# Eight of each layer's 24 gate projections traced between the two rounds of the RWKV inverse's merge

## The chip, the core and the metric

The kernel runs on one NeuronCore of a Trainium2 chip. The metric is the device time of one execution in microseconds (us). A profile shows one execution on the chip with the engines PE (TensorE matmuls), PEld (its weight loads), DVE (VectorE), ACT (ScalarE), POOL (GpSimd) and SP, which issues the DMAs.

## The reference

Two layers of a diffusion backbone with 512 tokens (256 context, 256 latent), model width 1024, float32. Each layer is a half-step SwiGLU, a token mixing, and a second half-step SwiGLU. The mixing is what matters here:

```python
cols = split(h @ w_in)                  # one projection feeds three branches and the gates
A = bidirectional retention(8 heads)    # "ret"
B = windowed attention(8 heads)         # "att"
C = bidirectional RWKV-7(8 heads)       # "rwkv", a scan with a state update per token
g = sigmoid(gate_logits)                # 3 x 1024 columns of the same projection
merged = g_ret * (ret @ w_ret) + g_att * (att @ w_att) + g_rw * (rwkv @ w_rwkv)
out = merged @ w_out
```

The gates depend on the normed input h alone. In layer 0 all 512 tokens are wanted; in layer 1 only the 256 latent ones, and the context enters only through states and keys.

## The kernel before

Activations lie with features on the partitions, so one 128-wide column block of a projection is a sum over eight 128x128 weight blocks. Each product is split in three (`mm3`: high weight by high and low activation, low weight by high activation), so a gate is 24 products, 512 columns wide in layer 0 and 256 wide in layer 1, into one of the two `mm` banks of PSUM. Then ACT takes the tanh (L589) and SP stores it to DRAM (L590, tile `gd`). `Weights.get` brings the weights in loads of four blocks; ACT rounds them (L114, `whi`, four buffers) and DVE subtracts for the low part (L115, `wlo`, three buffers).

The RWKV scan is done in chunks of 64 tokens, for four pairs of heads `p` and the two halves `s` (context 0, latent 1). Its steps have letters in the table `ORDER`, which gives the order in which the mixing is traced:

- `c`: the pair's columns r, k and v, with their convolution (on DVE), and the norm of k.
- `A` (s = 0) and `C` (s = 1): `rw_prep`. Its last score products (L976) give small triangular matrices. POOL inverts their 32x32 diagonal blocks in 62 instructions (L1008, L1009), after a trip through DRAM, and SP sends the result through DRAM (L1012 `td`).
- `B` (s = 0) and `D` (s = 1): `rw_back`, which first merges the 32x32 blocks into 64x64 inverses (`rw_merge`): it reloads the blocks (L1018, tile `z`), transposes and copies them on DVE (L1023, L1027) and ACT (L1026), multiplies in a first round of 16 products 32x32 (L1035), copies the result on ACT (L1036, tile `xm`), and multiplies in a second round of 16 (L1040). Then come `rw_vals` (L1052) and the chain of state updates `rw_chain` (L1079 to L1107): PE, ACT and DVE in turn, four steps in two directions, whose L1086 reads the merged inverse.

The other letters are `P` and `H` (retention: projections and heads), `kv`, `q`, `t` (attention), and `G`, two gates. Here `B0` of layer 0 is written 0B0, and so on. A scheduler takes the traced instructions, goes by their order as a priority, and puts an instruction whose inputs come late behind others whose inputs are there. Each engine then works through its queue in the order so made. `tc.issue_after(x)` orders what is traced inside it behind instruction `x` where both are on one engine.

Of the kernel before, what the change touches and what calls it, by code (L numbers as in the profile page):

```python
# [26 lines left out]
G3 = 3  # L27
# [3 lines left out]
def fm(src, n0, k=KT, k0=0):  # L31
    return [(src, kt, n0) for kt in range(k0, k0 + k)]


def grp(src, n0):
    return [(src, kt, n0 + j) for kt in range(KT) for j in range(2)]
# [15 lines left out]

ORDER = ['lo c0 A0 C0 B0 P0 kv c1 D0 H0 H1 q0 A1 t0 P1 t1 G0 C1 B1 H2 G1 c2 H3 G2 D1 A2 G3 q1 B2 P2 G4 C2 H4 t2 G5 t3 c3 A3 G6 H5 D2 G7 G8 P3 H6 G9 C3 B3 H7 D3 G10 G11', 'lo c0 A0 C0 P0 H0 kv B0 D0 c1 A1 H1 q0 t0 G0 t1 C1 G1 B1 P1 c2 D1 H2 A2 H3 P2 C2 G2 G3 H4 G4 c3 q1 G5 t2 t3 G6 B2 H5 D2 G7 A3 C3 G8 P3 B3 G9 G10 H6 H7 D3 G11']


def plan_mix(l):
    r0 = RCOL // 128
    out = []  # L60
    for w in ORDER[l].split():
        k, j = w[0], w[1:]
        if w == "lo":
            out.append(("lo", [("mix", kt, r0 + 12 + j) for kt in range(KT) for j in range(3)]))
            if l > 0:
                out.append(("vd", [("vd", 0, 0), ("vd", 0, 1)]))
        elif k == "c":
            p = int(j)
            out += [(f"r{p}", fm("mix", r0 + p)), (f"k{p}", fm("mix", r0 + 4 + p)), (f"v{p}", fm("mix", r0 + 8 + p))]
        elif k == "P":  # L70
            p = int(j)
            out += [(f"rq{p}", fm("mix", p)), (f"rk{p}", fm("mix", 4 + p)), (f"rv{p}", grp("mix", 8 + 2 * p))]
        elif k == "H":
            out.append((f"rg{j}", fm("mix", 16 + int(j))))
        elif w == "kv":
            out.append(("akv", grp("mix", 28)))
        elif k == "q":
            out.append((f"aq{j}", grp("mix", 24 + 2 * int(j))))
        elif k == "G":
            out += [(f"g{g}", fm("mix", 45 + g)) for g in range(2 * int(j), 2 * int(j) + 2)]  # L80
    for n in range(KT):
        out.append((f"ba{n}", fm("watt", n, 4)))
    out += [(f"br{n}", fm("wret", n)) for n in range(KT)]
    out += [(f"bw{n}", fm("wrw", n, 4)) for n in range(KT)]
    out += [(f"wo{n}", fm("wout", n)) for n in range(KT)]
    return out
# [36 lines left out]
def body(nc, tc, I, O, es, dbg=None):  # L123
# [3 lines left out]
    V, A, G, PE, SP = nc.vector, nc.scalar, nc.gpsimd, nc.tensor, nc.sync  # L127

    def mk(shape, tag, bufs=1, dt=F32):
        return sb.tile(shape, dt, name=tag, tag=tag, bufs=bufs)  # L130
# [3 lines left out]
    def ps(tag):  # L134
        return pp.tile([128, 512], F32, name="ps_" + tag, tag=tag, bufs=NB[tag])
# [4 lines left out]
    def ft():  # L140
        return mk([128, 512], "ft", 8)
# [7 lines left out]
    def span(S):  # L149
        return slice(S[0] * 256, S[-1] * 256 + 256)  # L150
# [34 lines left out]
    def mm3(o, w, h, start, stop):  # L185
        PE.matmul(o, w[0], h[0], start=start, stop=False)  # L186
        PE.matmul(o, w[0], h[1], start=False, stop=False)  # L187
        PE.matmul(o, w[1], h[0], start=False, stop=stop)  # L188

    def rsqrt(y, x):  # L190
        p, n = x.shape
# [14 lines left out]
    st = {"apart": False}  # L206
# [120 lines left out]
    def hl(h, c):  # L327
        return h[0][:, c], h[1][:, c]

    def dense(W, key, H, c, o):  # L330
        bl = W.take(key)
        for j, t in enumerate(bl):
            mm3(o[:, c], W.get(t), hl(H[j], c), j == 0, j == len(bl) - 1)

    def last_out(W, key, H, gate):

# [243 lines left out]
        SP.dma_start(out=st["od"][8 + h, :, c], in_=g[:, c])  # L580


    def gates(W, H, j, S, st):
        c = span(S)
        for g in range(2 * j, 2 * j + 2):
            o = ps("mm")
            dense(W, f"g{g}", H, c, o)
            t = ft()
            A.activation(t[:, c], o[:, c], AF.Tanh, scale=0.5)  # L589
            SP.dma_start(out=st["gd"][g, :, c], in_=t[:, c])  # L590

    def spilled(st, j, n, S, dst, mark, scale=None):
        c = span(S)
        for p in range(n):
            t = ft()
            with tc.issue_after(mark):
                SP.dma_start(out=t[:, c], in_=st["od"][j + p, :, c])
            split(hl(dst[p], c), t[:, c], scale)
        return dst
# [412 lines left out]
            SP.dma_start(out=td[:, :, g], in_=tt[g * 32:g * 32 + 32])  # L1012
        X["td"] = td

    def rw_merge(X, st):
        z, tn, xm = mk([64, 2, 8, 32], "z", 2), mk([32, 16, 32], "rb", 3)[:, 0:8], mk([64, 16, 32], "rb", 3)[:, 0:8]
        for b in range(2):
            mark = SP.dma_start(out=z[32 * b:32 * b + 32].rearrange("p d u t -> p (d u) t"), in_=X["td"][16 * b:16 * b + 16].rearrange("u j g i -> (j g) u i")).ins  # L1018
        st["marks"].append(mark)
        fl = lambda t: t.rearrange("p u t -> p (u t)")  # L1020
        tg = X["tg"]
        tu = [tg[d].rearrange("p h c t -> p (h c) t") for d in range(2)]
        V.transpose(fl(tn), fl(z[0:32, 0]))  # L1023
        for b in range(2):
            bs = slice(32 * b, 32 * b + 32)
            A.copy(tu[0][bs, :, bs], z[bs, 0])  # L1026
            V.transpose(tu[1][bs, :, bs], z[bs, 1])  # L1027

        o = ps("rx")
        ov, o2 = (o[:, j * 256:j * 256 + 256].rearrange("p (u x) -> p u x", x=32) for j in range(2))  # L1030
        ab = (slice(0, 32), slice(32, 64))
        for d in range(2):
            a, b = ab[d], ab[1 - d]
            for u in range(8):
                PE.matmul(ov[b, u], X["off"][a, u], tn[:, u] if d == 0 else z[a, 1, u], start=True, stop=True)  # L1035
        A.copy(xm, ov[0:64])  # L1036
        for d in range(2):
            a, b = ab[d], ab[1 - d]
            for u in range(8):
                PE.matmul(o2[a, u], xm[b, u], tu[d][b, u, b], start=True, stop=True)  # L1040
        V.tensor_copy(tu[0][ab[0], :, ab[1]], o2[ab[0]])
        A.copy(tu[1][ab[1], :, ab[0]], o2[ab[1]])

# [97 lines left out]
    def rw_front(l, p, s, S, st):  # L1141
        R, X = st["rw", p]
        rw_prep(l, p, s, R, st, s in S, X[s])

    def rw_back(l, p, s, S, st):
        R, X = st["rw", p]
        rw_merge(X[s], st)
        rw_vals(s, R, st, s in S, X[s])
        ya = rw_chain(l, p, s, R, st, s in S, s == 0, X[s])
        if s in S:  # L1150
            rw_out(l, p, s, R, st, ya, X[s])
            if p < 3:
                SP.dma_start(out=st["od"][p, :, CS[s]], in_=R["r"][:, CS[s]])
            else:
                st["last"] = R["r"]
# [20 lines left out]
    def mix(l, W, H, S, vf, mark, st):  # L1176
        c = span(S)
        st["mark"] = mark
        st["od"] = dp.tile([16, 128, 512], F32, name="od", tag="od", bufs=2)
        st["gd"] = dp.tile([24, 128, 512], F32, name="gd", tag="gd", bufs=2)  # L1180
        for w in ORDER[l].split():
            k, j = w[0], w[1:]
            if w == "lo":
                rw_lora(W, H, l, S, st)
            elif k == "c":
                st["rw", int(j)] = rw_cols(W, H, l, int(j), S, st, vf), [{}, {}]
            elif k in "AC":
                rw_front(l, int(j), "AC".index(k), S, st)
            elif k in "BD":
                rw_back(l, int(j), "BD".index(k), S, st)  # L1190
            elif k == "P":
                ret_proj(W, H, int(j), S, st)
            elif k == "H":
                ret_head(W, H, int(j), S, st)
            elif w == "kv":
                att_kv(W, H, st)
            elif k == "q":
                att_q(W, H, int(j), S, st)
            elif k == "t":
                att_pair(int(j), S, st)  # L1200
            elif k == "G":
                gates(W, H, int(j), S, st)
        return branches(W, S, st), st["mark"]

    def mix_out(l, W, ms, S, xd):
# [21 lines left out]
    for l in range(2):  # L1227
        S = both if l == 0 else lat
# [4 lines left out]
        if l == 0:  # L1233
# [3 lines left out]
            H = norm(0, 0, 0, both, fine)  # L1237
            tk = tasks(0, range(2, 9))
        else:
            H = norm(1, 0, 0, both)  # L1240
            ada_cond()
            tk = tasks(1, range(5, 9))
        W = Weights(nc, mk, I[f"w{l}a"], plan_ffn("f1i", "f1o"))
# [4 lines left out]
        H = norm(l, 1, 3, both)  # L1248
        xd = dp.tile([8, 128, 512], F32, name="xd", tag="xd", bufs=2)
        for kt in range(KT):  # L1250
            mark = SP.dma_start(out=xd[kt], in_=xs[kt]).ins
        W = Weights(nc, mk, I[f"w{l}b"], plan_mix(l), True)
        ms, mark = mix(l, W, H, S, vf, mark, mst)
        mix_out(l, W, ms, S, xd)
        H = norm(l, 2, 6, S)
# [5 lines left out]
        W = Weights(nc, mk, I[f"w{l}c"], plan_ffn("f2i", "f2o"))  # L1261
# [105 lines left out]
```

## Time and profile before

| | |
|---|---|
| time, median of 3 runs | 2948.22 us (2942.67 to 2951.27) |
| the profiled execution | 2950.47 us, its span 2948.7 us |
| PE busy | 2797.0 us (95%), 16761 matmuls |
| DVE, ACT, POOL busy | 2002.5, 1319.8, 376.2 us |
| mean granted TensorE clock | 0.963 of full speed |

The span is the time from the first to the last instruction of the profiled execution. PE is busy for 95% of it, but "busy" counts a matmul at half clock for twice as long. The mean of the granted clock, 0.963, says how much of the span ran at which of the two levels.

### The profile page before, as it was taken

To read this page: it belongs to the slowest core of one execution; us is meant where nothing else is said; L and a number is where in the kernel's file an instruction comes from. 1 tells how busy PE (TensorE), PEld (TensorE's weight loads), DVE (VectorE), ACT (ScalarE), POOL (GpSimd) and SP (SyncE) were. 2 spreads that over 40 slices of the span, in tenths; PEclk is the share of its full clock that TensorE was granted. 3 is DMA by queue.
4 is the path that set the end of the run, shared out by engine and by line. 5 is a ranking of instruction groups with operands and counts; after the bars stand their busy time and mean duration, and the time that the engine had idled before them with its cause. 6 is when DMAs were issued, how large, how long until landed. Compare 5 with 4: busy or idle time off the path is not lost. (4 is left out here: it accounts for less than half of the span.)

```text
span 2948.7 us, 47410 instructions
## 1 busy us (share of the span) xinstructions
PE 2797.0 (95%) x16761; PEld 2389.1 (81%) x16761; DVE 2002.5 (68%) x4677; ACT 1319.8 (45%) x2968; POOL 376.2 (13%) x1068
## 2 busy tenths in 40 slices
PE   7999999889999999999999999999989889899999
PEld 6888888767877787788888888888878788788999
DVE  7977668676676666566756466465787767678655
ACT  3322245556555654333223232233567665565544
POOL 0000000522132112000000000000033434330000
PEclk9999999789999999999999999999999888899999
DMA  7655534212333136534534435343433234246554
GB/s 267 232 189 183 163 122 130 83 39 82 111 97 89 49 123 207 176 102 147 195 114 169 147 111 185 104 164 122 137 90 108 75 110 116 61 124 212 170 179 154
DMA packets 259727, 400.97 MB, mean 136 GB/s; under 512 B 78752, under 2 KB 96288, under 8 KB 259488
## 3 DMA queue, kind: packets, MB, share of 16 engines
q1 hardware_dynamic: 259488, 397.93, 42.2%
q8 instruction: 132, 2.16, 0.3%
q14 instruction: 107, 0.88, 0.1%
HBM read 368.33 MB, written 25.82 MB: 134 GB/s over the span
## 5 line engine op out<-in xcount | busy, mean ns | idle before, releaser
L114 ACT CAST whi<-raw 128x512 fp32r<-128x512 f32 x954 | 564.1, 618 | 675.7 <-PE ps_mm L187 350.0
L186 PE MATMUL ps_mm<-hall,whi 128*128 128x512 f32 (+1 forms) x2320 | 845.1, 365 | 10.2 <-DVE rr_v L801 4.0
L188 PE MATMUL ps_mm<-hall,wlo 128*128 128x512 f32 (+1 forms) x2320 | 842.6, 364 | 2.0 <-DVE wlo L115 2.0
L187 PE MATMUL ps_mm<-hall,whi 128*128 128x512 f32 (+1 forms) x2320 | 840.8, 363 | 0.0
L115 DVE TENSOR_TENSOR wlo<-raw,whi 128x512 fp32r<-128x512 f32 x954 | 643.8, 691 | 104.3 <-ACT whi L114 68.3
L186 PEld LDWEIGHTS ps_mm<-hall,whi 128*128 128x128 f32 x2320 | 442.9, 191 | 80.6 <-ACT cst L981 4.4
L188 PEld LDWEIGHTS ps_mm<-hall,wlo 128*128 128x128 f32 x2320 | 441.6, 191 | 74.8 <-DVE wlo L115 4.1
L187 PEld LDWEIGHTS ps_mm<-hall,whi 128*128 128x128 f32 x2320 | 442.0, 191 | 71.4 <-issue 0.2
L186 PE MATMUL ps_mm<-hid,whi 128*128 128x512 f32 (+1 forms) x737 | 260.6, 354 | 0.0
L187 PE MATMUL ps_mm<-hid,whi 128*128 128x512 f32 (+1 forms) x737 | 259.9, 354 | 0.0
L188 PE MATMUL ps_mm<-hid,wlo 128*128 128x512 f32 (+1 forms) x737 | 257.3, 354 | 0.0
L1008 POOL TENSOR_TENSOR cst<-acc,cst 128x60 f32<-128x60 f32 (+24 forms) x496 | 172.4, 348 | 615.5 <-DMA acc<-ad__10934 59.2
L401 DVE TENSOR_TENSOR ft<-ft,ps_mm 128x512 f32<-128x512 f32 (+1 forms) x80 | 49.7, 621 | 210.4 <-PE ps_mm L188 198.1
L373 DVE SCALAR_TENSOR_TENSOR x<-ps_mm,cst,x 128x256 f32<-128x256 f32 x136 | 61.0, 480 | 193.1 <-PE ps_mm L188 193.1
L853 POOL TENSOR_TENSOR ll<-lora,lh 128x512 fp32r<-128x512 f32 x8 | 10.3, 1282 | 1359.2 <-DVE ft L300 942.6
L1009 POOL TENSOR_TENSOR cst<-cst 128x60 f32<-128x60 f32 (+24 forms) x496 | 176.2, 355 | 38.1
L236 DVE SCALAR_TENSOR_TENSOR ft<-m,cd 128x1024 bf16<-128x1024 f32 x136 | 163.0, 1221 | 9.8 <-DMA m<-ada 9.8
L237 DVE SCALAR_TENSOR_TENSOR m<-m,cd 128x1024 f32<-128x1024 f32 x136 | 165.4, 1221 | 0.7
L186 PEld LDWEIGHTS ps_mm<-hid,whi 128*128 128x128 f32 x737 | 139.1, 189 | 19.6
L187 PEld LDWEIGHTS ps_mm<-hid,whi 128*128 128x128 f32 x737 | 139.1, 189 | 19.4
L188 PEld LDWEIGHTS ps_mm<-hid,wlo 128*128 128x128 f32 x737 | 138.5, 189 | 19.4
L187 PE MATMUL ps_mm<-wlo,hall 128*128 128x256 f32 x416 | 122.6, 295 | 2.7 <-DVE wlo L115 2.6
(339 smaller groups left out, 4505.3 us busy)
## 6 DMA issues: line engine op xcount, KB each, us to landing
m<-ada SPq DMA_DIRECT2D x136, 512.0 KB, 4.4
raw<-w0b SPq DMA_DIRECT2D x214, 256.0 KB, 2.9
raw<-w1b SPq DMA_DIRECT2D x211, 256.0 KB, 3.2
raw<-w0a SPq DMA_DIRECT2D x132, 256.0 KB, 2.8
raw<-w0c SPq DMA_DIRECT2D x132, 256.0 KB, 4.5
raw<-w1a SPq DMA_DIRECT2D x132, 256.0 KB, 4.3
raw<-w1c SPq DMA_DIRECT2D x132, 256.0 KB, 3.9
gd<-ft SPq DMA_DIRECT2D x24, 256.0 KB, 2.0
```

The costliest lines, as they stand in the source:

```text
L114: nc.scalar.copy(hi, raw)
L115: nc.vector.tensor_sub(lo, raw, hi.bitcast(F32))
L186: PE.matmul(o, w[0], h[0], start=start, stop=False)
L187: PE.matmul(o, w[0], h[1], start=False, stop=False)
L188: PE.matmul(o, w[1], h[0], start=False, stop=stop)
L236: V.scalar_tensor_tensor(junk, raw, 1.0, st["cond"][0], ALU.mult, ALU.mult, accum_out=md[:, kt, 0:1])
L237: V.scalar_tensor_tensor(raw, raw, 1.0, st["cond"][1], ALU.mult, ALU.mult, accum_out=md[:, kt, 1:2])
L373: V.scalar_tensor_tensor(xs[n][:, CS[s]], o[:, CS[s]], gate[:, n, s:s + 1], xs[n][:, CS[s]], ALU.mult, ALU.add)
L401: V.tensor_tensor(sg[:, c], sg[:, c], pu[:, c], ALU.mult)
L853: G.tensor_sub(ll, lw, lh.bitcast(F32))
L1008: G.tensor_tensor(w, acc[j // 16][:, j % 16, j + 1:32].unsqueeze(1).to_broadcast([128, m, n]), tt[:, 0:m, j:j + 1].to_broadcast([128, m, n ...
L1009: G.tensor_tensor(tt[:, 0:m, j + 1:32], tt[:, 0:m, j + 1:32], w, ALU.add)
```

## The change

`ORDER` keeps eight `G` of twelve in each layer, now numbered 4 to 11: layer 0 loses the four that stood at G0, G2, G5 and one of G7 and G8; layer 1 loses those at G0, one of G2 and G3, G5 and G7 (the numbers before). The gates 0 to 7 go to the merges: `rw_merge` calls `gate()` between its two rounds, which traces one gate's 24 products with its tanh and its store, and the second round is traced under `issue_after` of the last of these products. The order of the weights in DRAM (`plan_mix`) follows.

```diff
+        elif k in "GBD":
+            gs = range(2 * int(j), 2 * int(j) + 2) if k == "G" else [2 * int(j) + "BD".index(k)]
+            out += [(f"g{g}", fm("mix", 45 + g)) for g in gs]
...
-    def gates(W, H, j, S, st):
+    def gates(W, H, gs, S, st):
         c = span(S)
-        for g in range(2 * j, 2 * j + 2):
+        for g in gs:
             o = ps("mm")
-            dense(W, f"g{g}", H, c, o)
+            ins = dense(W, f"g{g}", H, c, o)
...
+        return ins
...
-    def rw_merge(X, st):
+    def rw_merge(X, st, gate):
...
         A.copy(xm, ov[0:64])
-        for d in range(2):
-            a, b = ab[d], ab[1 - d]
-            for u in range(8):
-                PE.matmul(o2[a, u], xm[b, u], tu[d][b, u, b], start=True, stop=True)
+
+        mark = gate()
+        with tc.issue_after(mark):
+            for d in range(2):
+                a, b = ab[d], ab[1 - d]
+                for u in range(8):
+                    PE.matmul(o2[a, u], xm[b, u], tu[d][b, u, b], start=True, stop=True)
...
-        rw_merge(X[s], st)
+        rw_merge(X[s], st, lambda: gates(W, H, [2 * p + s], S, st))
```

Two places in PE's queue show what the scheduler makes of it. The first is the merge 0B0. Before, these rows stand around its two rounds (`ps_rx<-rb,cst` and `ps_rx<-z,cst` are round one, `ps_rx<-tg,rb` round two, L976 the score products of 0C0, L559 a retention head):

```order
L188 MATMUL ps_mm<-whi,hall 128x256
L976 MATMUL ps_rf<-arz,kb 128x256 x2
L1035 MATMUL ps_rx<-rb,cst 32x32 x8
L1035 MATMUL ps_rx<-z,cst 32x32 x8
L1052 MATMUL ps_rx<-cst,rr_v 128x128 x2
L559 MATMUL ps_po<-ft 128x128 x2
L1040 MATMUL ps_rx<-tg,rb 32x32 x16
```

The rows 128x256 into `ps_mm` are the attention's query columns (q0); 48 of them stand ahead of round one. With the change, round one of 0B0 (now L1038) stands here, with the lines six numbers on (L561 for L559, L979 for L976):

```order
L979 MATMUL ps_rf<-arz,kb 128x256 x2
L188 MATMUL ps_mm<-hall,whi 128x512
L189 MATMUL ps_mm<-hall,wlo 128x512
L561 MATMUL ps_po<-ft 128x128 x2
L550 MATMUL ps_sc<-rqh,rks 128x512
L551 MATMUL ps_sc<-rql,rks 128x512
L979 MATMUL ps_rf<-arz,kb 128x256 x2
L1038 MATMUL ps_rx<-rb,cst 32x32 x8
L1038 MATMUL ps_rx<-z,cst 32x32 x8
L1058 MATMUL ps_rx<-cst,rr_v 128x128 x2
L187 MATMUL ps_mm<-whi,hall 128x256
```

No q0 product stands ahead of round one any more, and 32 of them stand between the rounds; the gate that 0B0 itself traces stands some 450 rows ahead, and that of 0D0 some 100 rows ahead.

The second place is the merge 1B2 in layer 1. Before, its two rounds follow each other, split only by score products of 1C2:

```order
L1134 MATMUL ps_rx<-cst,rb 128x64 x4
L1135 MATMUL ps_rx<-lo,cst 128x256
L1035 MATMUL ps_rx<-rb,cst 32x32 x8
L1035 MATMUL ps_rx<-z,cst 32x32 x8
L1040 MATMUL ps_rx<-tg,rb 32x32 x6
L976 MATMUL ps_rf<-arz,kb 128x256 x2
L1040 MATMUL ps_rx<-tg,rb 32x32 x10
```

With the change this is round one and what follows it (the products 128x512 are columns of pair 3):

```order
L1140 MATMUL ps_rx<-cst,rb 128x64 x4
L1141 MATMUL ps_rx<-lo,cst 128x256
L1038 MATMUL ps_rx<-rb,cst 32x32 x8
L1038 MATMUL ps_rx<-z,cst 32x32 x8
L979 MATMUL ps_rf<-arz,kb 128x256 x2
L187 MATMUL ps_mm<-hall,whi 128x512
```

and this is round two, 160 rows further on (the products into `ps_mm` ahead of it are the end of 1B2's gate):

```order
L737 MATMUL ps_ap<-cst,ft 128x128 x3
L189 MATMUL ps_mm<-hall,wlo 128x256
L187 MATMUL ps_mm<-hall,whi 128x256
L188 MATMUL ps_mm<-hall,whi 128x256
L189 MATMUL ps_mm<-hall,wlo 128x256
L1046 MATMUL ps_rx<-tg,rb 32x32 x16
```

Between them stand 24 products of 512 columns and 122 of 256, three gates among them.

## Rows read from the trace of the kernel before

**Rows 1.** The span by stretch (windows): busy time of each engine, granted clock, DMA.

```profile
410.00:1240.00 830.00, 772.11 (x4825) 641.47 (x4825) 569.94 (x1530) 438.36 (x1085) 183.84 (x532) 0.94 0.34 103
...
2065.00:2715.00 650.00, 588.84 (x4422) 517.04 (x4421) 477.84 (x1300) 393.06 (x996) 192.15 (x532) 0.92 0.38 112
```

**Rows 2.** Line L1040, the second round: what its engine sat idle for, times.

```profile
  ACT rb L1036: 1.0, 2
```

**Rows 3.** Tile z: what engines sat idle for, and who waited (us, times).

```profile
  DMA z<-td: 112.6, 33
...
  ACT tg L1026: 61.7, 19
```

**Rows 4.** Timeline of 0B0, from the last score product of 0A0 to round one.

```profile
509.11 1.02 PE L976 MATMUL ps_rf<-arz,kb 128*128 128x256 f32 x4
...
552.45 1.18 SPq L1018 DMA_DIRECT2D z<-td  x2
...
556.66 0.83 ACT L1026 COPY tg<-z 32x256 f32<-32x256 f32 x2 [10.66 <-DMA z<-td]
...
558.08 0.90 PE L1035 MATMUL ps_rx<-rb,cst 32*32 32x32 f32 x13 [7.57 <-DVE rb L1023]
```

**Rows 5.** Windows behind that wait, and of layer 1's worst stretch: columns as in rows 1.

```profile
560.00:580.00 20.00, 19.39 (x122) 17.94 (x123) 10.84 (x47) 9.26 (x32) 10.30 (x33) 0.57 0.27 73
...
558.00:616.00 58.00, 49.73 (x312) 42.31 (x312) 41.17 (x145) 32.22 (x94) 20.98 (x66) 0.71 0.20 55
...
2388.00:2460.00 72.00, 66.68 (x443) 59.74 (x442) 46.02 (x127) 41.52 (x108) 22.39 (x66) 0.82 0.36 103
```

**Rows 6.** Timeline of PE: the other stalls behind a late z.

```profile
881.61 0.68 PE L1107 MATMUL ps_rx<-ve,tg 64*64 64x64 f32 x4 [3.56 <-ACT ve L1088]
...
2197.86 0.56 PE L1035 MATMUL ps_rx<-rb,cst 32*32 32x32 f32 x13 [1.56 <-DVE rb L1023]
...
2328.89 0.55 PE L186 MATMUL ps_mm<-hall,whi 128*128 128x256 f32 x1 [4.01 <-DVE rr_v L801]
...
2383.65 0.56 PE L1035 MATMUL ps_rx<-rb,cst 32*32 32x32 f32 x13 [1.19 <-DVE rb L1023]
2387.48 1.22 PE L1052 MATMUL ps_rx<-cst,rr_v 128*128 128x128 f32 x4 [2.76 <-ACT kbT L958]
...
2518.47 0.66 PE L1079 MATMUL ps_rx<-cst,gk 128*64 128x128 f32 x2 [5.79 <-DVE cst L1102]
```

**Rows 7.** Timeline of PE: products in a row at full clock, and a head's.

```profile
511.01 0.48 PE L548 MATMUL ps_sc<-rqh,rks 128*128 128x512 f32 x1
...
511.56 0.28 PE L908 MATMUL ps_rf<-lw,lh 128*128 128x256 f32 x1
...
544.96 1.95 PE L559 MATMUL ps_po<-ft 128*128 128x128 f32 x16
...
548.42 0.28 PE L186 MATMUL ps_mm<-whi,hall 128*128 128x256 f32 x1
548.54 0.28 PE L187 MATMUL ps_mm<-wlo,hall 128*128 128x256 f32 x1
...
749.22 0.39 PE L186 MATMUL ps_mm<-hall,whi 128*128 128x512 f32 x1
749.45 0.39 PE L187 MATMUL ps_mm<-hall,whi 128*128 128x512 f32 x1
```

**Rows 8.** Timeline of DVE and POOL late in the inverse for 1D2.

```profile
2500.10 0.68 DVE L115 TENSOR_TENSOR wlo<-raw,whi 128x512 fp32r<-128x512 f32 x1
...
2500.11 0.84 POOL L1008 TENSOR_TENSOR cst<-acc,cst 128x65 f32<-128x65 f32 x1
...
2502.50 0.31 POOL L1008 TENSOR_TENSOR cst<-acc,cst 128x66 f32<-128x66 f32 x1
```

**Rows 9.** Timeline of PE around 1B2: round one and the chain's first step on the inverse.

```profile
2462.85 0.59 PE L1035 MATMUL ps_rx<-rb,cst 32*32 32x32 f32 x13
...
2487.61 0.44 PE L1086 MATMUL ps_rx<-cst,tg 64*64 64x64 f32 x4
```

More of the change, by code (lines that the diff above doesn't have):

```diff
@@ L49, in plan_ffn @@
     return out
-ORDER = ['lo c0 A0 C0 B0 P0 kv c1 D0 H0 H1 q0 A1 t0 P1 t1 G0 C1 B1 H2 G1 c2 H3 G2 D1 A2 G3 q1 B2 P2 G4 C2 H4 t2 G5 t3 c3 A3 G6 H5 D2 G7 G8 P3 H6 G9 C3 B3 H7 D3 G10 G11', 'lo c0 A0 C0 P0 H0 kv B0 D0 c1 A1 H1 q0 t0 G0 t1 C1 G1 B1 P1 c2 D1 H2 A2 H3 P2 C2 G2 G3 H4 G4 c3 q1 G5 t2 t3 G6 B2 H5 D2 G7 A3 C3 G8 P3 B3 G9 G10 H6 H7 D3 G11']
+ORDER = ['lo c0 A0 C0 B0 P0 kv c1 D0 H0 H1 q0 A1 t0 P1 t1 C1 B1 H2 G4 c2 H3 D1 A2 G5 q1 B2 P2 G6 C2 H4 t2 t3 c3 A3 G7 H5 D2 G8 P3 H6 G9 C3 B3 H7 D3 G10 G11', 'lo c0 A0 C0 P0 H0 kv B0 D0 c1 A1 H1 q0 t0 t1 C1 G4 B1 P1 c2 D1 H2 A2 H3 P2 C2 G5 H4 G6 c3 q1 t2 t3 G7 B2 H5 D2 A3 C3 G8 P3 B3 G9 G10 H6 H7 D3 G11']
 def plan_mix(l):
@@ L78, in plan_mix @@
             out.append((f"aq{j}", grp("mix", 24 + 2 * int(j))))
-        elif k == "G":
-            out += [(f"g{g}", fm("mix", 45 + g)) for g in range(2 * int(j), 2 * int(j) + 2)]
+        elif k in "GBD":
+            gs = range(2 * int(j), 2 * int(j) + 2) if k == "G" else [2 * int(j) + "BD".index(k)]
+            out += [(f"g{g}", fm("mix", 45 + g)) for g in gs]
     for n in range(KT):
@@ L187, in mm3 @@
         PE.matmul(o, w[0], h[1], start=False, stop=False)
-        PE.matmul(o, w[1], h[0], start=False, stop=stop)
+        return PE.matmul(o, w[1], h[0], start=False, stop=stop).ins
     def rsqrt(y, x):
@@ L332, in dense @@
         for j, t in enumerate(bl):
-            mm3(o[:, c], W.get(t), hl(H[j], c), j == 0, j == len(bl) - 1)
+            ins = mm3(o[:, c], W.get(t), hl(H[j], c), j == 0, j == len(bl) - 1)
+        return ins
     def last_out(W, key, H, gate):
@@ L590, in gates @@
             SP.dma_start(out=st["gd"][g, :, c], in_=t[:, c])
+        return ins
     def spilled(st, j, n, S, dst, mark, scale=None):
@@ L1143, in rw_front, with rw_back @@
         rw_prep(l, p, s, R, st, s in S, X[s])
-    def rw_back(l, p, s, S, st):
+    def rw_back(W, H, l, p, s, S, st):
         R, X = st["rw", p]
-        rw_merge(X[s], st)
+        rw_merge(X[s], st, lambda: gates(W, H, [2 * p + s], S, st))
         rw_vals(s, R, st, s in S, X[s])
@@ L1189, in mix @@
             elif k in "BD":
-                rw_back(l, int(j), "BD".index(k), S, st)
+                rw_back(W, H, l, int(j), "BD".index(k), S, st)
             elif k == "P":
@@ L1201, in mix @@
             elif k == "G":
-                gates(W, H, int(j), S, st)
+                gates(W, H, range(2 * int(j), 2 * int(j) + 2), S, st)
         return branches(W, S, st), st["mark"]
```

## The prediction

> **What bounds the kernel now.** I began with the busy time by stretch. TensorE is the bound nearly everywhere; only the two mixings leave it idle, 830 − 772.1 = 58 us in layer 0 and 650 − 588.8 = 61 us in layer 1, and there alone the mean granted clock is clearly under 1, at 0.94 and 0.92 [rows 1]. No product is added or taken away, so the change can win or lose only within these 119 us and in what the clock costs.
>
> Then I asked what the second round, which the change moves, waits for. The reader should see that it waits for almost nothing: ACT's copy L1036, the input that a gate between the rounds could cover, costs 1.0 us in the whole kernel [rows 2]. What engines do wait for in a merge stands ahead of both rounds: the reloaded blocks `z`, 112.6 us of idle time over all engines, 61.7 of it on ACT alone [rows 3]. Most of that is hidden from TensorE, but not all. At 0B0 the last score product leaves at 509.11, `z` is issued at 552.45, ACT's copy has waited 10.66 us for it and TensorE 7.57 us when round one starts at 558.08 [rows 4]. So 49 us pass, and where TensorE's own queue holds less than that, it stops.
>
> The remaining stalls of this kind are in the timeline: 3.56 (chain of 0B2), 1.56 (1B0), 4.01 (ahead of 1B1), 1.19 and 2.76 (1D1), 5.79 (the chain of the pair before, waiting for DVE, which stands at 1D2's `z`) [rows 6]. With the 7.57 they make 26.4 us. These are what the change can move: a gate placed ahead of round one is cover for `z`, one between the rounds or elsewhere is not.
>
> **The change part by part.** Moving eight gates per layer moves 24 products each, two roundings on ACT, two subtractions on DVE, a tanh and a store. Their count stays, so their own cost is nothing; they lie under TensorE's queue, and the store's tile `gd` is read only after the mixing.
>
> *The second round's new wait.* By name the change makes round two wait for a gate. In the order of the changed kernel the gate stands between the rounds in two of 16 merges, 0B3 and 1B2; in the other 14 it was put far ahead and round two is free at once. In 0B3 both kernels hold much work between the rounds. In 1B2 round two and what is queued behind it (`rw_vals`, the chain's first read of the inverse, L1086) come later: before, round one stood at 2462.85 and L1086 at 2487.61 [rows 9]; now 63 more products of 256 columns stand ahead of L1086, counted from 1A2's last score product, at 0.12 us (548.42 to 548.54) [rows 7], so 7.6 us. The chain itself loses the same 63 as cover (88 before, 25 now). Its end moves by nothing if that cover was not needed, and by up to 7.6 us if all of it was. I take 2.0, near the low end, since four steps still have some 20 us of attention products between them.
>
> *The cover of `z`.* I counted what stands between a merge's last score product and its round one, before and now, with prices at full clock: 0.23 us for 512 columns (749.22 to 749.45), 0.12 for 256, 0.55 for the pair L548/L549 (511.01 to 511.56), 1.95 / 16, about 0.11 less overlap, for L559 [rows 7].
> - 0B0: 23 more products of 512 (+5.3), 48 of 256 gone (−5.8), ten L559 gone (−1.1), three pairs gone (−1.65), small ones −0.4: 3.7 us less cover, so the wait of 7.57 grows to about 11.3.
> - 1B0: 18 products of 256 more and one pair less, +1.7: its 1.56 disappears.
> - 1B1: four pairs and eight L559 gone, 3.0 less; the stall of 4.01 grows by that.
> - 1D1: 75 products of 256 gone (−9.0), three pairs and eight L559 more (+2.5), small ones −0.4: 6.9 less; 1.19 becomes about 8.
> - 1D2: on DVE, whose wait matters here, `z` is met 3.7 us of TensorE work later, so 5.79 shrinks by 3.7.
> - 0B2: ACT meets `z` 7.2 us later, so its 3.56 disappears.
> - 1D3: 19 products of 256 less, 2.5 in all, against a present wait of under half a us: +2.5.
>
> *What is given back.* A product that leaves a cover stands somewhere else, and if it falls where TensorE idles, the wait that grew is paid back. Behind 0B0 there is plenty of room: from 558 to 616 us TensorE is busy 49.73 of 58, at a clock of 0.71 [rows 5], and the order puts 48 more products of 256 and ten more L559 here. 48 × 0.12 + 10 × 0.11 = 6.9 against 8.3 idle: I take all of the 3.7 as returned. Behind 1D1, 2388 to 2460 idles 5.3 of 72 us [rows 5]; I take half of 1D1's loss as returned, and half for 1B1 and 1D3, where no row decides between nothing and all.
>
> The sum: 0B0 0, 1B0 −1.6, 1B1 +1.5, 1D1 +3.5, 1D2 −3.7, 0B2 −3.6, 1D3 +1.3, 1B2 +2.0, together −0.6 us. The profiled execution took 2950.47 us, so 2949.9; it lies 2.25 above the median of the runs, so 2947.6, and I say 2948. That is no change: about 0.3%, or 8.8 us, is what a measurement of this kernel tells from none.
>
> **A rule weighed against the trace.** Late in an inverse POOL's 128x65 product took 0.84 us beside a subtraction L115 of 0.68, while a 128x66 one alone took 0.31 [rows 8]. So a gate's two L115 falling into an inverse could make its `z` later by 2 × 0.53, or at most by 2 × 0.68 = 1.4 us. The Trainium skill, "SBUF — State Buffer", section "SBUF: two separate sides", says that a VectorE operation with two SBUF inputs and a GpSimd operation hold their shared ports exclusively, the later one standing still for the whole instruction. By that rule 0.84 is nearly one L115 of waiting plus 0.31, and the trace agrees. Were each of 0B0, 1D1 and 1D3 to get 1.4, the sum would be −0.6 + 4.2, or 2952 instead of 2948. Subtractions of other columns fill those stretches in both kernels, so I do not add it.
>
> **The rivals.**
> - *Faster: the waits that grew are returned in full, and the clock stays up.* The three gains are 1.6 + 3.7 + 3.6 = 8.9, so 2939. Besides, behind 0B0's wait the clock falls: 560 to 580 has 0.57, with TensorE busy 19.39 [rows 5]. At 0.57 a share of 0.86 lies at the half level, and 19.39 × 0.86 / 2 = 8.3 us is what it costs. If the denser work there keeps the clock at 2.4 GHz, 2931. I take 2935. What speaks for it is that this stretch gets more products; against it, that the wait ahead of it is longer, and after such an idle time the clock fell. It decides at whether the granted clock in the 20 us behind 0B0's round one is above 0.8.
> - *Slower: nothing is returned.* Then 3.7 − 1.6 + 3.0 + 6.9 − 3.7 − 3.6 + 2.5 + 7.6 = +14.8, so 2963. The place is layer 1, where 1B2's chain hangs behind three gates: its late end makes the next pair's products late, and they stand ahead of 1D2's. For it speaks that the idle in 2388 to 2460 is in pieces, waits of chains among them, which a product from elsewhere doesn't fill. It decides at 1B2's chain ending more than about 4 us later against the work around it.
> - *The change doesn't do what it says:* the second round hardly waited and in 14 merges the gate isn't between the rounds. Then what remains is a re-ordering of gates, and the mechanisms above are all there is. I hold this as true in any case; it is why I forecast no change.
>
> **How the numbers follow.** No change, 2948, has a chance of 0.40; its own range, with each half returned between nothing and all, is 2939 to 2957. The faster rival has 0.33, the slower 0.27: the order was reshuffled at 14 places, and every term is a few us with either sign, so neither is far behind. From 2930 to 2963 the range takes in the full price of both rivals.
>
> **What would show it.** In the changed profile, round one of 0B0 should wait about 11 us (7.57 before), that of 1D1 about 8, and 1B0's 1.56, the 3.56 in 0B2's chain and most of the 5.79 should be gone. The second round (L1046) should still wait for next to nothing, also in 1B2, where it follows round one by some 25 us. TensorE's busy time at full clock must be the same. I am wrong if the idle time in the two mixings differs from 58 + 61 by more than 9 us, if the clock in either one moves by 0.02 (some 13 us), or if waits appear at other places than those listed, for instance at casts L114 held up in ACT's queue behind a `z` that now stands earlier among them.

## The result

The changed kernel takes 2973.33 us (median of 4 runs, 2966.28 to 2974.58) against 2948.77 before: a ratio of 1.0081, 95% interval 1.0059 to 1.0104. It is slower by 24 us, where no change was forecast, and outside the range of 2930 to 2963. Its profiled execution has a span of 2970.7 us.

The windows of the two mixings, cut at this kernel's own ends, answer to [rows 1] (columns as there):

```profile
410.00:1247.00 837.00, 784.90 (x4822) 652.94 (x4823) 570.02 (x1520) 432.50 (x1083) 185.22 (x532) 0.93 0.34 101
2074.00:2733.00 659.00, 580.59 (x4395) 510.64 (x4394) 471.93 (x1289) 388.26 (x993) 194.00 (x532) 0.92 0.38 111
```

Layer 0's mixing is 7 us longer, with 52 us of idle time instead of 58, so it lost to the clock. Layer 1's two windows do not end at the same place of the program. From the first score product (L976, now L979) to the last product of the RWKV output (L1135, now L1141) both do the same products:

```profile
2147.20:2710.20 563.00, 510.55 (x3909) 448.25 (x3908) 410.18 (x1135) 344.94 (x903) 186.95 (x525) 0.92 0.38 111
```

```profile
2156.20:2733.00 576.80, 507.28 (x3908) 446.80 (x3908) 407.63 (x1135) 341.62 (x903) 188.82 (x525) 0.92 0.38 108
```

The first line is before, the second after: 13.8 us longer, with 69.5 us idle instead of 52.5. The end of it moved by 23 us in all.

What the second round waits for, and what engines wait for at `z`, first looks unchanged. This is the line of the second round, as [rows 2]:

```profile
  ACT rb L1039: 1.8, 4
```

And this is tile `z`, as [rows 3], its time as a whole and who stood there:

```profile
  DMA z<-td: 116.0, 36
...
  ACT tg L1029: 56.5, 19
  DVE tg L1030: 36.8, 11
  DVE rb L1026: 22.6, 6
```

112.6 became 116.0 us (93.1 in a second execution, experiment 5, so this total says little by itself). But TensorE is hit harder by the same standing. These are its long stalls behind a late `z` in the timeline, as [rows 4, 6]:

```profile
559.80 0.87 PE L1038 MATMUL ps_rx<-rb,cst 32*32 32x32 f32 x13 [5.16 <-DVE rb L1026]
...
2211.68 1.22 PE L561 MATMUL ps_po<-ft 128*128 128x128 f32 x4 [7.01 <-DVE ft L558]
...
2270.80 0.41 PE L1038 MATMUL ps_rx<-rb,cst 32*32 32x32 f32 x8 [3.69 <-DVE rb L1026]
...
2352.16 0.87 PE L1038 MATMUL ps_rx<-rb,cst 32*32 32x32 f32 x13 [8.98 <-DVE rb L1026]
...
2475.61 0.69 PE L1140 MATMUL ps_rx<-cst,rb 64*128 64x64 f32 x4 [6.74 <-DVE rb L1137]
...
2528.28 1.97 PE L779 MATMUL ps_po<-kv,aT 128*128 128x64 f32 x8 [7.69 <-ACT aT L777]
```

Added over all TensorE stalls that fall together with an engine standing at `z`, layer 1 has 37.6 us where it had 18.2, and the rest of its idle time is the same (60.2 − 18.2 = 42.0 before over 57 gaps of the timeline, 79.7 − 37.6 = 42.1 after over 61). The second execution has 32.0 us of such stalls, and stalls of 2.2 to 9.7 us at the same six places. The stall ahead of 1B0's round one shows how. This is VectorE's queue there:

```profile
2198.91 0.42 DVE L489 TENSOR_SCALAR dt<-ph,cst 128x384 f32<-128x384 f32 x1
2207.30 0.43 DVE L1030 STREAM_TRANSPOSE tg<-z 32x256 f32<-32x256 f32 x1 [7.97 <-DMA z<-td]
...
2211.21 0.42 DVE L558 TENSOR_TENSOR ft<-ps_sc,dt 128x256 f32<-128x256 f32 x1
```

VectorE stands 7.97 us at its head, at `z`. Behind it in the same queue, at 2211.21, stands L558, the decay product of a retention head, and TensorE's L561 needs it. That head stands ahead of round one in TensorE's queue, so TensorE stops at it at once, 7.01 us, with nothing in between that could cover the wait.

### The profile page after: what moved, and what is told of

Same layout as the page of the kernel before. It is cut to its first block, busy times and chain, and to the rows that moved or that the text cites. A ratio compares the mean times of both kernels' runs of the same rounds, so it can differ in the third digit from the quotient of the medians.

```text
span 2970.7 us, 47425 instructions
## 1 busy us (share of the span) xinstructions
PE 2803.9 (94%) x16761; PEld 2395.9 (81%) x16761; DVE 1998.1 (67%) x4677; ACT 1303.0 (44%) x2968; POOL 380.0 (13%) x1068
## 4 chain that ended last, share of the span: by engine, by line
PE 59%; POOL 7%; DVE 6%; DMA 4%; ACT 2%; issue 2%; SPq 1%; POOLq 0%; DVEq 0%; ACTq 0%
PE ps_mm L188 15%; PE ps_mm L187 15%; PE ps_mm L189 15%; POOL cst L1012 4%; POOL cst L1011 3%; PE ps_rf L979 1%; DVE wlo L116 1%; DMA z<-td 1%; PE ps_po L779 1%; PE ps_rx L1092 1%; PE ps_rx L1085 1%; PE ps_mm L366 1%; PE ps_po L561 1%; PE ps_rx L1038 1%; PE ps_rx L1113 1%
## 5 line engine op out<-in xcount | busy, mean ns | idle before, releaser
L115 ACT CAST whi<-raw 128x512 fp32r<-128x512 f32 x954 | 556.7, 616 | 296.0 <-PE ps_mm L188 145.1
L1011 POOL TENSOR_TENSOR cst<-acc,cst 128x60 f32<-128x60 f32 (+24 forms) x496 | 172.5, 348 | 595.1 <-DMA acc<-ad__10854 56.1
L1012 POOL TENSOR_TENSOR cst<-cst 128x60 f32<-128x60 f32 (+24 forms) x496 | 175.6, 354 | 38.0
L211 ACT CAST hid<-ft 128x512 fp32r<-128x512 f32 (+1 forms) x88 | 50.0, 568 | 280.2 <-DVE ft L403 280.0
```

Source lines behind the costliest of these rows:

```text
L115: nc.scalar.copy(hi, raw)
L211: A.copy(dst[0], src)
L1011: G.tensor_tensor(w, acc[j // 16][:, j % 16, j + 1:32].unsqueeze(1).to_broadcast([128, m, n]), tt[:, 0:m, j:j + 1].to_broadcast([128, m, n ...
L1012: G.tensor_tensor(tt[:, 0:m, j + 1:32], tt[:, 0:m, j + 1:32], w, ALU.add)
```

## The experiments

Each is the changed kernel with the edit shown, unless it says otherwise. Ratios are to the kernel before, runs of the same chip.

**1. Without the tie.** The gate is traced where it was; only the tie of the second round goes.

```diff
-        mark = gate()
-        with tc.issue_after(mark):
-            for d in range(2):
+        gate()
+        for d in range(2):
```

> The changed kernel with the gate still traced between the two rounds, but the second round no longer tied behind it. Theory A: the loss comes from the new order of the gates around the merges, since engines stand longer at the reloaded blocks z; the tie touches only what follows 0B3, and TensorE waits there for nothing of it. A expects 2963 to 2975 us, at most 10 us under the changed kernel. Theory B: the tie costs, because the second round and the chain behind it come late in 0B3 and 1B2. B expects about 2949 to 2955.

2944.12 us, ratio 0.9981 (0.9966 to 0.9997). Theory A, which I held, falls: the gates in their new places cost nothing; the whole loss comes with the tie. Theory B, that the tie costs, named the cause but expected 5 us more than was measured. This is also the version that stands best against both kernels, if by little.

**2 and 3. One layer at a time.** `ORDER`, the plan of the weights and the merges of one layer as changed, of the other as before.

```diff
-        elif k in "GBD":
+        elif k == "G" or k in "BD" and NEW[l]:
...
-        rw_merge(X[s], st, lambda: gates(W, H, [2 * p + s], S, st))
+        rw_merge(X[s], st, (lambda: gates(W, H, [2 * p + s], S, st)) if NEW[l] else None)
```

> Layer 0 in the changed order with its ties, layer 1 as before. In the profile of the changed kernel layer 0's mixing ends 7 us later and layer 1's starts 9 us later than before. If the layers are independent (theory A) this kernel takes 2955 to 2959 us. If the tie of the second round is the cause (theory B), it is layer 1's 1B2 that pays and this one takes 2946 to 2952.

> Layer 1 in the changed order with its ties, layer 0 as before. In the changed profile layer 1's mixing takes some 14 us more than before, 10 of them before 1B0's round one. Theory A expects 2960 to 2966 us with the 7 us stall at the retention head ahead of 1B0's round one in it. Theory B expects the loss at 1B2 alone, so 2953 to 2960 and no gain if 1B0 were mended.

Layer 0 alone: 2946.25 us, 0.9994 (0.9979 to 1.0009). Layer 1 alone: 2952.23 us, 1.0013 (0.9997 to 1.0028). Each has its tie, and neither loses measurably. Both theories had expected more for layer 1 alone (2953 at the least), and A more for layer 0 (2955 at the least). The two don't add up to 24 us, so the loss needs both layers as changed: something passes from layer 0 to layer 1.

**4. The retention head ahead of the merge.** In layer 1's `ORDER`:

```diff
-... kv B0 D0 c1 A1 H1 q0 ...
+... kv H1 B0 D0 c1 A1 q0 ...
```

> The changed kernel with retention head H1 of layer 1 traced ahead of B0, so that all four of its products with the decay (L558) stand ahead of 1B0's z in VectorE's queue. Theory A in its sharp form: the 7.0 us stall at 1B0 is there because the moved gates pushed the head's products behind the z on VectorE; it goes, and the time is 2962 to 2968 us. In its loose form: z is late whatever stands behind it, TensorE then stops at round one instead for about as long, and the time stays at 2969 to 2976.

2961.22 us, 1.0042 (1.0026 to 1.0058): some 13 us of the loss are gone, as the sharp form said (by 1 us more than it allowed). VectorE's queue now has the four L558 ahead of `z`, and the stall at L561 is gone:

```profile
2202.96 0.42 DVE L558 TENSOR_TENSOR ft<-ps_sc,dt 128x256 f32<-128x256 f32 x1
...
2208.29 0.43 DVE L1026 STREAM_TRANSPOSE rb<-z 32x256 f32<-32x256 f32 x1 [1.58 <-DMA z<-td]
```

TensorE waits 1.14 us at round one instead:

```profile
2208.86 0.56 PE L1038 MATMUL ps_rx<-rb,cst 32*32 32x32 f32 x13 [1.14 <-DVE rb L1026]
```

So the way in which a late `z` reaches TensorE is right for this stall. That the 13 us are its doing isn't shown: the whole order of layer 1 changes with the head, and in experiment 8 the same move makes a kernel slower.

**5 to 7. The changed kernel again, and the tie in one layer.** With `st["tie"]` set to `l == 0` or to `l == 1`:

```diff
-        with tc.issue_after(mark):
+        with tc.issue_after(mark) if st["tie"] else nullcontext():
```

In the order of the instructions the tie binds in two places, 0B3 and 1B2; so these two and experiment 1 make a square of four kernels. Behind 0B3's round one, TensorE's queue without the tie is

```order
L1058 MATMUL ps_rx<-cst,rr_v 128x128 x2
L1046 MATMUL ps_rx<-tg,rb 32x32 x16
L561 MATMUL ps_po<-ft 128x128 x2
```

and with it L1046 stands nearly 60 rows further on. Up to this L1058 all four have the same queues. Those with the tie at 0B3 share all further ones up to 1B2's round one, those without it share theirs.

> The changed kernel once more, on the chip of the next three runs. If its loss belongs to the kernel, it takes 2966 to 2975 us here too; if part of it was that one chip, less.

> The second round is tied behind the gate in layer 0 alone. By the order of the instructions the tie binds at 0B3 only, and through it the scheduler arrives at another order for layer 1; up to 1B2 every engine's queue is that of the changed kernel. Theory D: the tie at 0B3 costs by this other order, in which engines stand at z and TensorE behind them (1B0 7.0, 1D0 3.7, 1B1 9.0 us). D expects 2962 to 2973 us. Theory B2: the late second round of 1B2 costs. B2 expects 2944 to 2952.

> The second round is tied behind the gate in layer 1 alone; the tie binds at 1B2 only, and up to there every queue is that of the kernel without ties. Theory D (the tie at 0B3 costs, through the order of layer 1) expects 2942 to 2949 us, about the kernel without ties. Theory B2 (the second round of 1B2 and its chain come late) expects 2958 to 2972.

The changed kernel: 2974.84 us, 1.0087 (1.0067 to 1.0107). Tie at 0B3 alone: 2957.33, 1.0033 (1.0021 to 1.0045). Tie at 1B2 alone: 2944.49, 0.9991 (0.998 to 1.0002). Theory D had the place right and the size wrong: the tie at 0B3 costs 13 us, that at 1B2 costs 0.4 us alone, and 17.5 us more on top of the first. The kernel without ties ran on another chip than these three; by the ratios, each to the kernel before on its own chip, the three prices are 15, 3 and 16 us. The profiled executions, cut at the first score product L979 of each layer, at round one of 0B3 and 1B2, and at the last L1141 (the last product of the RWKV output) of layer 0 (us):

| stretch | before | no tie | tie 1B2 | tie 0B3 | both |
|---|---|---|---|---|---|
| start to layer 0's first scores | 486.9 | 494.5 | 495.7 | 494.5 | 494.5 |
| to round one of 0B3 | 583.1 | 575.5 | 575.3 | 574.5 | 580.5 |
| to the end of layer 0's RWKV | 169.7 | 165.8 | 163.1 | 173.2 | 171.7 |
| to layer 1's first scores | 907.5 | 911.2 | 909.4 | 911.6 | 909.5 |
| to round one of 1B2 | 315.6 | 302.0 | 305.5 | 322.2 | 320.8 |
| to the end | 485.9 | 490.4 | 489.0 | 479.5 | 493.7 |
| span | 2948.7 | 2939.4 | 2938.0 | 2955.5 | 2970.7 |

Counted in the traces, a stretch up to 1B2 holds the same products in the four changed kernels, within half a microsecond's worth. The kernel before shares them out differently: ahead of layer 0's first scores it has 15,872 columns fewer, which at 0.23 us for 512 are 7.1 us.

The tie at 0B3 costs in two stretches. The first lies directly behind it, 7.4 us. There round two comes late, at 1097.86 in the changed kernel, 23.1 us after round one at 1074.77:

```profile
1074.77 0.59 PE L1038 MATMUL ps_rx<-rb,cst 32*32 32x32 f32 x13
...
1097.86 1.09 PE L1046 MATMUL ps_rx<-tg,rb 32*32 32x32 f32 x32
```

Without the tie it follows after 4.0 us:

```profile
1070.44 0.59 PE L1038 MATMUL ps_rx<-rb,cst 32*32 32x32 f32 x13
...
1074.41 1.09 PE L1046 MATMUL ps_rx<-tg,rb 32*32 32x32 f32 x32
```

The second is in layer 1, a thousand us later, up to 1B2's round one: 20.2 us, where no tie binds in either kernel. Of the two together, 10.9 us come back behind 1B2's round one (479.5 against 490.4). Two windows of the kernel without ties, the stretch behind 0B3 and that one:

```profile
1070.00:1235.80 165.80, 157.65 (x897) 126.44 (x895) 90.83 (x217) 62.70 (x162) 20.38 (x62) 0.95 0.47 154
...
2147.00:2449.00 302.00, 271.14 (x2028) 236.53 (x2026) 232.44 (x660) 195.35 (x513) 112.62 (x331) 0.94 0.36 101
```

The same two with the tie at 0B3, and then what follows 1B2's round one up to the last L1141:

```profile
1069.00:1242.20 173.20, 164.09 (x896) 130.33 (x895) 90.41 (x216) 63.07 (x161) 21.05 (x62) 0.92 0.45 148
...
2153.80:2476.00 322.20, 280.09 (x2035) 244.69 (x2035) 234.53 (x668) 195.45 (x517) 114.01 (x331) 0.89 0.34 94
2476.00:2707.30 231.30, 220.92 (x1762) 195.24 (x1760) 162.51 (x445) 142.32 (x378) 70.86 (x194) 0.93 0.42 127
```

Read the first column against the length. Behind 0B3 both idle 8 to 9 us; the clock is 0.92 instead of 0.95. So the late round two doesn't make TensorE idle for longer: most of the 7 us are products at the lower clock level, and what in the new order brings that about isn't shown. In layer 1 the idle time is 322.2 − 280.1 = 42.1 against 302.0 − 271.1 = 30.9 us, and the clock 0.89 against 0.94. Here the order is the one in which TensorE meets a head's L561 ahead of 1B0's round one while VectorE has its L558 behind `z`. Without ties round one comes first, and the head's product behind it waits for nothing:

```profile
2204.19 0.90 PE L1038 MATMUL ps_rx<-rb,cst 32*32 32x32 f32 x13
...
2206.86 1.06 PE L561 MATMUL ps_po<-ft 128*128 128x128 f32 x4
```

The tie binds in layer 0, and the scheduler, which places each instruction by the times it reckons with, seems to come to layer 1 at other reckoned times and so orders it otherwise; this reason is argued from the orders, not shown.

With both ties the 10.9 us don't come back: the last stretch takes 493.7 us. These are the windows of the changed kernel from 1B2's round one:

```profile
2477.00:2732.70 255.70, 232.50 (x1878) 207.32 (x1876) 173.19 (x470) 146.53 (x387) 73.22 (x194) 0.93 0.42 124
2732.70:2970.70 238.00, 228.59 (x1868) 227.24 (x1866) 141.65 (x282) 110.02 (x222) 0.00 (x0) 0.98 0.51 171
```

It idles 23.2 us in the first of them (20.0 in its second execution), with the tie at 0B3 alone 10.4, and 32.6 us to the end. With the tie at 0B3 alone, whose last L1141 comes with fewer products ahead of it, it is 17.8 to the end:

```profile
2707.30:2955.50 248.20, 240.78 (x1982) 240.06 (x1980) 156.70 (x306) 114.89 (x231) 0.00 (x0) 0.99 0.54 173
```

ScalarE shows the largest piece, 1D2, in the changed kernel

```profile
2527.35 0.40 ACT L1029 COPY tg<-z 32x256 f32<-32x256 f32 x1 [6.14 <-DMA z<-td]
2527.66 0.57 ACT L777 COPY aT<-ps_ap 128x512 f32<-128x512 f32 x1
```

where the attention's copy L777 stands behind `z` and TensorE's L779 waits 7.69 us for it, and with the tie at 0B3 alone

```profile
2522.35 0.41 ACT L1029 COPY tg<-z 32x256 f32<-32x256 f32 x1 [2.08 <-DMA z<-td]
...
2525.03 0.58 ACT L777 COPY aT<-ps_ap 128x512 f32<-128x512 f32 x1
```

where ScalarE waits 2.08 us and TensorE has no stall over 2.4 us at this place. (The kernel without ties has a stall of 5.53 us at L779 there and isn't slow, so this piece alone does not decide.)

**8. Without ties, the head ahead.** Experiments 1 and 4 together, the partner of 4.

> The kernel without ties, and retention head H1 of layer 1 traced ahead of B0: the partner of the kernel with ties and H1 ahead, which took 2961. Theory D: the loss is in one order that came out badly, not in the tie as such. Then this kernel has no reason to stand at the same distance under its partner (29 us): anything from 2938 to 2965 agrees. If ties cost as such, wherever they stand, it takes 2930 to 2942.

2954.94 us, 1.0026 (1.0013 to 1.004). The tie's price on this order is 2961.22 − 2954.94 = 6.3 us instead of 31, and the head that mended the kernel with ties makes the one without 11 us slower. In its profiled execution layer 1 takes 322 us from the first scores to 1B2's round one, where the kernel without ties and with the old place of the head takes 302 (some 5 of these 20 us are products that moved there), and 7 us more are lost in layer 0 ahead of 0B3, where the two have the same queues. So a head moved ahead of a merge is no remedy by itself.

**9 to 11. The blocks early.** GpSimd's inverse is cut to its first 8 steps, in the kernel before, the changed one and the one without ties:

```diff
-        for j in range(31):
+        for j in range(8):
```

> The kernel before, with only 8 of the inverse's 31 steps on GpSimd, so the blocks z are ready some 20 us earlier; the inverse, and with it the output, is not the reference's. Theory F: what the variants differ by is TensorE idle while engines stand at a late z (before: 12.6 us in layer 0, 18.2 in layer 1). F expects 2915 to 2932 us. If z were hidden anyway, 2944 to 2952.

> The changed kernel with the same 8 steps (the same part of the inverse left out). By the order the ties bind at 0B3 and 1B2 as before, but layer 1's queues up to 1B2 are now those of the kernel without ties. Theory F: of the loss of 26 us only what the late second round costs directly is left, 4 to 10 us over the kernel without ties and with the short inverse, so 2915 to 2935. Theory B (the ties cost directly, behind them the chains): still 20 us or more over its partner without ties.

> The kernel without ties, with the same 8 steps (the same part of the inverse left out). Theory F: 2910 to 2926, since its own idle time beside a standing z is 12.7 us in layer 0 and 15.7 in layer 1. It and the short kernel before should lie within 9 us of each other if the moved gates are neutral once z is early.

Before: 2894.77 us, 0.9812 (0.9777 to 0.9847). Changed: 2908.43, 0.9864 (0.984 to 0.9889). Without ties: 2903.0, 0.9845 (0.9825 to 0.9866). Earlier blocks give each kernel far more than F expected, 54, 66 and 41 us, so that all three lie under its ranges, and the tie's price shrinks from 31 to 5.4 us, inside F's 4 to 10. In the short pair layer 1's queues are the same up to 1B2 with and without ties, but for a few neighbours that change places; behind 1B2 they differ. Directly behind 0B3 the tie costs nothing here (163.8 against 163.4 us, round two again 23.3 us after round one). So a second round 23 us late is no loss as such. Of the changed kernel's stalls in layer 0 beside a standing `z`, 13.5 us, 1.8 are left. In the kernel before, the time at `z` fell from 112.6 to

```profile
  DMA z<-td: 76.5, 37
```

and the clock of the two mixings' windows, cut at 410 to 1240 and 2060 to 2720 us, is 0.94 and 0.96, where [rows 1] have 0.94 and 0.92:

```profile
410.00:1240.00 830.00, 784.75 (x4909) 654.25 (x4910) 576.27 (x1548) 443.47 (x1102) 56.92 (x164) 0.94 0.35 107
...
2060.00:2720.00 660.00, 619.59 (x4809) 550.35 (x4808) 501.13 (x1368) 417.76 (x1052) 55.41 (x162) 0.96 0.41 122
```

## Why the prediction was wrong

**What bounds the kernel** was right: no product was added, and nearly all of the loss lies in the two mixings: the same products take 7.0 us longer up to the end of layer 0's RWKV, 2.0 more to layer 1's first scores, and 13.8 in layer 1's mixing. In layer 1 it is idle time, mainly at late blocks `z`; in layer 0 it is the clock, for which the sum had no term. That `z` matters was, if anything, put too low: 26.4 us of named stalls against 41 to 66 us that the earlier blocks give back.

**The step that failed is "the second round's new wait".** It priced the tie by its two places, nothing at 0B3 and 2.0 us (at most 7.6) at 1B2. The square of experiments 1, 5, 6 and 7 has 13 us for 0B3 alone, 0.4 for 1B2 alone and 31 for both. At 0B3 the reason given, that both kernels hold much work between the rounds, was true of the kernel before and hid that the tie holds round two back 23 us where it could have followed after 4; the stretch behind it is 7.4 us longer. At 1B2 the estimate was good for that tie by itself, though round two follows round one by 31 us and not by 25. What no step held is that a tie binds at one place and is paid in the next layer, 20 us of it up to 1B2, through the order that comes out there.

**"The cover of z" counted the wrong distance**, and this is where the sum itself went wrong in layer 1. The prediction had the changed kernel's order in hand, layer 1's included, and could have seen its price there. Its terms for layer 1 (1B0, 1B1, 1D1, 1D2 and 1D3) add up to +1.0 us; measured are 18.2 us of stalls beside a standing `z` before and 37.6 after. It took the products up to round one, and found 1.7 us more cover at 1B0, so its 1.56 us would go. But VectorE and ScalarE also work in order: cover ends at the first product fed by anything that stands behind `z` in their queues. At 1B0 that is L561, and it waited 7.01 us. 1D2 shows the same on ScalarE, 7.69 us where 5.79 was to shrink. 1B1, to grow by 3.0, went from 4.01 to 8.98; 1D0, not listed, has 3.69; 1D1, forecast at 8, has no stall of note. At 0B0 round one waits 5.16 us, not 11.3. There the cover shrank, but the way from the last score product to round one did as well, which the term took as fixed. That score product now starts at 515.24, so round one at 559.80 comes 44.6 us after it, where it was 49.0:

```profile
515.24 1.02 PE L979 MATMUL ps_rf<-arz,kb 128*128 128x256 f32 x4
```

Of the seven terms 0B2 alone came out as said: the 3.56 is gone. The error of single terms is as large as the terms.

**"What is given back"** was half right. From the first scores to 0B3 the changed kernel is 2.6 us shorter than before, though 7,424 columns more (3.3 us) stand there; and the 7.6 us by which it starts them later are 7.1 us of products that were moved ahead. So up to 0B3 nothing was lost, as said. What layer 0 loses, it loses behind 0B3, at the lower clock.

**The net of the moved gates, no change, was right,** for the part that it described: without ties it is 0.9981, with the head moved 1.0026, and with early blocks 2903.0 against 2894.8. These lie at or within 0.3% to both sides. There is luck in it: the terms that cancel in the sum mostly did not come as forecast.

**The rivals.** "Slower" named 1B2's chain and 14.8 us; measured are 24 us, and the chain's lateness is free by itself (experiment 7). "The change doesn't do what it says" was taken as true and harmless: the gate does stand between the rounds in only two merges, but these two are what costs. The rule on the shared ports predicted 2952 through a longer inverse, but the inverse's two lines did not get longer: 172.5 and 175.6 us (L1011, L1012) after 172.4 and 176.2 before. The Trainium skill, "SBUF — State Buffer", "SBUF: two separate sides", says that the one of the two operations that comes later is blocked until the first is done, so subtractions too should get shorter when GpSimd's steps are cut. The trace agrees in direction, and it is little: in experiment 9 their mean went from 691 to 686 ns over 954 of them, 5 us in all. The row that the prediction took for the rule bears it out only in part: 0.68 + 0.31 = 0.99 us, and the product took 0.84.

**What stays open.** Why the tie at 1B2 costs 17.5 us on one order and 0.4 on the other is located only in part: 15 us more idle time behind 1B2's round one, the largest piece at 1D2. With it goes what the order with the tie at 0B3 alone had won back there. That 1D2's stall is its cause was not tried by itself, and some 6 us of the difference between the two profiles lie ahead of 0B3, where no tie has bound yet. What lowers the clock behind 0B3 is open too. That the scheduler's reckoned times carry the tie's effect into layer 1 is argued from the orders; that a changed order came and cost is shown. The short inverse also takes work off GpSimd and changes the order, so its 54 us are not the price of late blocks alone.

## What to carry to other kernels

A tie or a moved instruction in a scheduled program has two prices: what waits behind it, and the order that all later work comes out in. Compare the orders up to the end, not only around the edit, and switch each tie off by itself before believing in a local cause. Compare also stretches in which the queues are the same: what differs there isn't the edit's doing, and here that was up to 9 us. For a late transfer, count the cover to the first product that depends on anything behind it in any in-order queue, not to its own consumer.

## What the runs showed that was not expected

The four kernels of the square have the same queues up to 0B3's round one; three take 574.5 to 575.5 us from the first scores to there, and the changed kernel took 580.5 and, in experiment 5, 580.1. Two of these 5 us are in the wait at 0B0 (5.16 and 5.05 us against 2.9 to 3.7); the rest has no explanation here. It is not the ties: the kernels of experiments 4 and 8 have the same queues up to there as well, one with ties and one without, and both take some 583 us. So differences of a few us between two of these kernels, like the 5.4 and 6.3 above, can't be put down to a tie.

Cutting GpSimd's inverse took 54 us off the kernel before, of which its profile had shown only 30.8 us as idle time beside a standing `z`. TensorE's busy time fell as well, from 2797.0 to 2771.9 us, with the same products: with fewer stalls there was also less time at the lower of the two clock levels, a mean granted clock of 0.971 where it was 0.963.
